# Moving GpSimd's two-operand elementwise work in the second block to VectorE, and the gates' factor on the one-hot rows to ScalarE

## The chip, the cores and the metric

The program runs on one core of one Trainium2 chip. The metric is device time in microseconds (us) for one launch, the median of several runs. The engines are named as in the profile: PE is TensorE (its matmuls; its weight loads are PEld), DVE is VectorE, ACT is ScalarE, POOL is GpSimd, SP is SyncE.

## What is computed

Two transformer blocks in float32 on 256 tokens of width 2048, one after the other. The change touches only the second. It has a mixer (retention and a gated recurrence behind one input product), an attention to 256 memory rows, and a product-key expert layer, cut here to what matters:

```
q  = rmsnorm(h) @ w_q                       # 8 heads x 2 halves of 128
s1 = q1 @ sub_keys1, s2 = q2 @ sub_keys2    # 128 keys each
best 16 of each, best 16 of their sums      # per token and head
gate = softmax over the 16
act  = gelu(rmsnorm(h) @ U)                 # all 16384 experts
h   += (act * gates of all experts) @ V
```

The 128 gates of a token (8 heads x 16) stand in a matrix of 128 x 128 experts: the kernel builds it, token by token, as a product of two one-hot matrices, of which the first is multiplied by the gates.

## The kernel before, in words

Every large product streams its weights. `Stream.run` (L139) goes through all half pieces of weights (128 x 1024 values) in program order. At half piece i, `ahead` (L90) first issues the load of a later piece on SP's queue and the split of half piece i + 4: `split` (L77) has ACT round the raw weights to float32r (`whi`, L84) and another engine take the difference (`wlo`, L87). Then PE gets the matmuls of half piece i (L163 to L165, or L173 and L174 where the weights are stationary), and `steps(2)` (L118) lets the tasks in `side` emit one step each, two steps in all (a step that yields "pause" is not counted). So the order of each engine's queue is fixed when the program is built: split of half i + 4, matmuls of half i, then a little of the other work. Each engine takes its queue in order.

The difference of L87 is VectorE's, except where a product was added with the key `pool`: there every second, third or fourth half piece is GpSimd's. That holds for six of the twelve products behind `w_in_2` (`block2`, 24 half pieces), for the four of `w_q` (`peer`, 16 half pieces), and for the first eight of `peer_u` (17 half pieces), 57 in all.

Three more places use GpSimd for a product or a sum of two tensors in SBUF:

- `normed` (L1461) builds the normalised operand of the experts in eight parts: a sum (L1467) and a product with the row of norms (L1468), 128 x 512 each, then ACT and VectorE split it (L1470, L1471).
- `topk` (L1495), once for each of four pairs of heads, finds the best keys on VectorE (MAX8, FIND_INDEX8, MATCH_REPLACE8) and at its end compares places with 0 to 15 (`eq`, L1552, VectorE) and multiplies by the indices (L1554, GpSimd), 4 x 2 x 4 = 32 times 128 x 256, before a sum (L1558).
- `gates` (L1561) goes through 64 groups of four tokens. `hot(k)` makes the two one-hot matrices `oh` of group k, 128 x 512 each, by two comparisons on VectorE (L1583) and one multiplication of the first by the gates on GpSimd (L1585). In the loop, group k + 2 is made, then PE multiplies group k (L1599, four products of 128 x 128), ACT writes the result to `gst` (L1601), and after every fourth group GpSimd issues two stores to DRAM (L1604). Three groups come in two half pieces. Beside it runs the product `peer_u`, whose end for every four half pieces is `gelu_pair` (L1444): one step on ACT and one on VectorE in each of three half pieces (L1450 and L1451, L1453 and L1454, L1456 and L1457).

Behind the gates, `weigh` (L1610) reads them back from DRAM, multiplies the activations by them (L1626) and splits the product (L1629, L1630), four parts for each sixteenth of the experts.

GpSimd's other work is small: `rsqrt` (L236), one cast in `topk` (L1510), and issuing DMAs.

Of the kernel before, what the change touches and what calls it, by code (L numbers as in the profile page):

```python
# [42 lines left out]
class Stream:  # L43
    """The weight products: pieces of weights are loaded ahead, split ahead into two float32r parts
    whose sum is exact, and multiplied in order, with the steps of other work put in between."""
# [11 lines left out]
    def add(s, **j):  # L57
        """A product: pieces (weights, their blocks of 128 rows, columns, part of the product)."""
        parts = [piece[3] for piece in j["pieces"]]
        for c, piece in enumerate(j["pieces"]):  # L60
            p, u = len(s.pieces), piece[3]
            s.pieces.append(piece[:3])
            nk = len(piece[1])
            cuts = [0, nk] if nk * piece[2] <= 1024 else [0, nk // 2, nk]
            for k0, k1 in zip(cuts, cuts[1:]):
                s.halves.append((j, p, k0, k1, c == 0 and k0 == 0, u, u not in parts[:c] and k0 == 0,
                                 u not in parts[c + 1:] and k1 == nk))
# [9 lines left out]
    def split(s, i):  # L77
# [7 lines left out]
        # where VectorE has much else to do, GpSimd takes a part of the differences  # L85
        e = s.nc.gpsimd if "pool" in j and i % j["pool"] == 0 else s.nc.vector
        e.tensor_tensor(lo[:, :w], raw, hi[:, :w].bitcast(F32), op=ALU.subtract)  # L87
        s.parts[i] = (hi, lo)

    def ahead(s, i):  # L90
        """Loads and splits as far ahead of half piece i as there is room."""
# [8 lines left out]
    def spawn(s, *gens, first=False):  # L100
        """Other work, after the task that is running or before all."""
# [3 lines left out]
    def step(s, g):  # L105
        """One step of a task: whether it did something."""
# [11 lines left out]
    def steps(s, n):  # L118
        """A step each of the first n tasks that have something to do."""
# [61 lines left out]
class Kernel:  # L181
# [16 lines left out]
    def g(self, shape, name, dt=F32):  # L198
        """A tile of the shared store, of at most 4 KB of a partition."""
# [16 lines left out]
    def keep1(self, shape, name):  # L216
        """1 KB of a partition that is kept for long, but not for all of the time."""
# [12 lines left out]
    def rsqrt(self, out, ss, n, eps=EPS):  # L230
        """out = (ss / n + eps) ** -0.5"""
# [6 lines left out]
    def row_bcast(self, out, r, late=1):  # L238
        """A task: out[p, t] = r[t % 128, t // 128] on every partition."""
# [11 lines left out]
    def sumsq(self, out, x, n):  # L251
        """out[p] = the sum of x squared along the free axis."""
# [3 lines left out]
    def turned(self, dst, src, kbs, gain=None):  # L256
        """dst[:, hi/lo, i, tok], the transposed [128 tok, 128] blocks src(m, kb) of two kbs, times
        gain(kb) by row, in two exact parts."""
# [19 lines left out]
    def wparts(self, name, c, late=False):  # L278
        """Of 512 columns, two parts of 256, for a product with the weights stationary; in turns
        where the last rows of the operand come late."""  # L280
# [22 lines left out]
    def attention(self, q, k, bias, v, done, start=None, sums=None, then=None):  # L303
        """q(h, m), k(h, keys), v(h, kt), bias(h, m) give operands; done(m, h0, nh, po, rs) takes the
        products of the unnormalised probabilities and one over their sums, to which sums may add;
        the task then() follows."""
# [50 lines left out]
    def group(self, g, o):  # L357
        """The group norm of o [128, m, 512], into two operand tiles of the next product."""
# [40 lines left out]
    def both(self, o, y, z, scale=1.0):  # L399
        """The two parts of a product with the weights stationary, added."""  # L400
# [3 lines left out]
    def end_w(self, name, scale, R):  # L404
        """The end of a product with the weights stationary: [n, tok] times scale times R by column."""
# [10 lines left out]
    def end_t(self, name, r):  # L416
        """The end of a product with the tokens stationary: [tok, n] times r by row."""
# [8 lines left out]
    def block1(self):  # L426
# [83 lines left out]
        # memory keys and values, kept in DRAM until they are needed  # L510
# [23 lines left out]
    def rel_bias(self):  # L534
        """The relative bias and the masks: bias[h // 4][q, h % 4, j] for the key at distance
        128 + q - j, and the one of the compressed keys."""
# [14 lines left out]
        # the compressed keys lie at distances of which those of the keys are a part, or in the future  # L551
# [23 lines left out]
    def mla_prep(self):  # L575
# [13 lines left out]
        # the rotated shared key  # L589
# [55 lines left out]
    def log1p_exp_neg(self, y, n):  # L645
        """log1p(y) for y in [0, 1], as 2 artanh(y / (2 + y)) by its series, in place."""
# [15 lines left out]
    def log_sigmoid(self, out, z, n):  # L662
        """out = min(z, 0) - log1p(exp(-|z|))"""
# [9 lines left out]
    def fox_gate(self):  # L673
        """The running sums of the gates' logarithms along the tokens, by token and transposed."""
# [77 lines left out]
    def gelu(self, out, x, w, half=True):  # L752
        """out = 2 gelu(x), or gelu(x) with half, for x [128, w] in PSUM or not (tanh form)."""
# [9 lines left out]
    def nsa(self):  # L763
# [8 lines left out]
        for kv in range(2):  # L772
            # the keys (values) of the blocks, flat, and their positions' (in the last column), times
            # the first weights: one product a position, for both groups, one below the other
# [40 lines left out]
        # the gates  # L815
# [5 lines left out]
        # the compressed keys  # L821
# [45 lines left out]
        # the selected blocks (four of four: all of them up to the query), and the window  # L867
# [43 lines left out]
    def residual_end(self, n, src, gain, dst, then=None):  # L911
        """The end of a product whose n-th 512 columns add to h; the new h is squared, and turned
        for the next product with its gain."""
# [98 lines left out]
    def second_norm(self, n, h, hg):  # L1012
        """The first block's last norm and the second's first: hg = h * final_norm is what both
        square, and what the next product takes, with its own gain."""
# [37 lines left out]
    def block2(self):  # L1052
# [48 lines left out]
        for i, (mode, c, end) in enumerate(jobs):  # L1101
            pieces = self.wparts("w_in_2_w", c) if mode == "w" else self.wpieces("w_in_2_t", c)
            more = {"begin": lambda: S.side.extend([self.tables(), self.lru(), self.retention(0), self.retention(1)])}
            S.add(mode=mode, pieces=pieces, x=x, need=need, end=end, **({"pool": 2} if 3 <= i < 9 else {}),
                  **(more if i == 0 else {}))

    def rotate(self, d, name, c, u, y, z):
        """The rotary turn of a product with the weights stationary, and its norm."""
# [16 lines left out]
    def gelu_y(self, c):  # L1125
        """2 gelu of the gate of the recurrence, in place."""
# [78 lines left out]
    def lam(self):  # L1205
        """8 log_sigmoid(lambda), by channel."""
# [180 lines left out]
    LAG = 4  # L1387

    def peer(self):
# [14 lines left out]
        for c in range(4):  # L1404
            S.add(mode="w", pieces=self.wparts("w_q", c, c == 0), x=lambda kb: (self.fT[kb // 2], kb % 2), end=q_end(c),
                  pool=2,
# [27 lines left out]
        for s in range(16 + self.LAG):  # L1434
            if s < 16:
                for u in (2 * s, 2 * s + 1):
                    S.add(mode="w", pieces=self.wparts("peer_u", u), x=lambda kb: (self.fn[kb // 2], kb % 2),
                          end=u_end(u), **({"pool": 3 if u < 2 else 4} if u < 8 else {}),
                          need=lambda kbs: kbs[-1] // 2 in self.fn,
# [4 lines left out]
    def gelu_pair(self, c, u, y, z):  # L1444
        """2 gelu of a part of a product, in turns between the engines."""
# [15 lines left out]
    def normed(self):  # L1461
        """The normalised operand of the experts."""
        nc = self.nc
        yield from self.wait("Rf")
        for e in range(8):
            t, o, x = self.fT[e], self.xe("fn"), self.w([128, 2, 256], "fx")
            nc.gpsimd.tensor_tensor(x, t[:, 0].bitcast(F32), t[:, 1].bitcast(F32), op=ALU.add)  # L1467
            nc.gpsimd.tensor_tensor(x, x, self.Rf[:, None, :].to_broadcast([128, 2, 256]), op=ALU.mult)  # L1468
# [6 lines left out]
    def top16(self, rows):  # L1475
        """For each (v, idx, s): v, idx become the 16 largest of s along the free axis, in order, and
        their places; s is changed. The rows go side by side."""
# [17 lines left out]
    def topk(self, c, q):  # L1495
        """The sixteen best of two heads' product keys, for all tokens."""
# [14 lines left out]
        # the pairs that can be among the best sixteen: with a and b better ones in the two lists,  # L1511
# [171 lines left out]
def _col(v):  # L1683
    """[n * 128] -> [128, n]"""
    return v.reshape(-1, 128).T
# [36 lines left out]
def _rotary():  # L1722
    """cos and sin for the transposed [channel, token] heads of 128, for queries and for keys."""
    half = 64
# [100 lines left out]
```

## Time and profile before

| what | value |
|---|---|
| median of 3 runs | 3584.61 us (3584.1 to 3586.18) |
| profiled execution, its span (first to last instruction) | 3584.7 us |
| PE busy | 3495.4 us (98%) |
| PEld busy | 2965.4 us (83%) |
| DVE busy | 2348.0 us (66%) |
| ACT busy | 1647.2 us (46%) |
| POOL busy | 388.8 us (11%) |
| mean granted TensorE clock | 0.993 |
| HBM traffic | 186 GB/s over the span |

No separate time is given for the profiled execution beside its span, which lies 0.1 us above the median of the runs. A busy share is a mean over stages that differ: POOL is near 0 in most of the span and at 5 to 6 tenths from about 1950 to 2330 us, the same stretch in which DVE is at 9 tenths and PE falls below 9. Busy time of an engine counts an instruction from its start to its end, so it holds what the instruction waited for after its start.

### The profile page before, as it was taken

To read this page: it belongs to the slowest core of one execution; us is meant where nothing else is said; L and a number is where in the kernel's file an instruction comes from. 1 tells how busy PE (TensorE), PEld (TensorE's weight loads), DVE (VectorE), ACT (ScalarE), POOL (GpSimd) and SP (SyncE) were. 2 spreads that over 40 slices of the span, in tenths; PEclk is the share of its full clock that TensorE was granted. 3 is DMA by queue.
4 is the path that set the end of the run, shared out by engine and by line. 5 is a ranking of instruction groups with operands and counts; after the bars stand their busy time and mean duration, and the time that the engine had idled before them with its cause. 6 is when DMAs were issued, how large, how long until landed. Compare 5 with 4: busy or idle time off the path is not lost.

```text
span 3584.7 us, 45859 instructions
## 1 busy us (share of the span) xinstructions
PE 3495.4 (98%) x18204; PEld 2965.4 (83%) x18204; DVE 2348.0 (66%) x3371; ACT 1647.2 (46%) x2298; POOL 388.8 (11%) x319
## 2 busy tenths in 40 slices
PE   9999999999999999999999888899999999999998
PEld 8888888888888888788888677778888888888887
DVE  5565565545555566875556999966666666666765
ACT  5455445444343454445444344444444444444443
POOL 0000000000000002310005556600000000000000
PEclk9999999999999999999999999999999999999999
DMA  6444455555555554455545445655555555555654
GB/s 220 166 143 165 174 189 178 193 188 199 185 197 198 195 197 180 153 176 187 191 153 179 138 157 184 195 205 200 200 200 200 201 201 203 203 202 202 222 210 153
DMA packets 103351, 670.28 MB, mean 187 GB/s; under 512 B 11684, under 2 KB 12469, under 8 KB 30176
## 3 DMA queue, kind: packets, MB, share of 16 engines
q1 hardware_dynamic: 87120, 610.98, 47.8%
q0 software_dynamic: 15728, 56.29, 4.8%
q8 instruction: 143, 2.34, 0.3%
q14 instruction: 72, 0.59, 0.0%
q10 hardware_dynamic: 288, 0.07, 0.0%
HBM read 644.21 MB, written 23.09 MB: 186 GB/s over the span
## 4 chain that ended last, share of the span: by engine, by line
PE 76%; DVE 13%; issue 6%; ACT 2%; POOL 2%; DMA 0%; POOLq 0%; SPq 0%; DVEq 0%; ACTq 0%
PE mm L173 21%; PE mm L163 13%; PE mm L165 13%; PE mm L164 13%; PE mm L174 11%; DVE wlo L87 4%; ACT whi L84 2%; DVE wx L1626 2%; DVE oh L1583 2%; POOL oh L1585 1%; PE ss L315 1%; PE ss L263 1%; PE ss L342 1%; DVE ti L1486 0%; DVE acc L1419 0%
## 5 line engine op out<-in xcount | busy, mean ns | idle before, releaser
L87 DVE TENSOR_TENSOR wlo<-raw,whi 128x1024 fp32r<-128x1024 f32 (+2 forms) x1105 | 1376.4, 1265 | 439.1 <-ACT whi L84 438.0
L84 ACT ACTIVATE whi<-raw 128x1024 fp32r<-128x1024 f32 (+2 forms) x1162 | 1196.6, 1049 | 546.4 <-PE mm L165 473.2
L173 PE MATMUL mm<-xT,whi 128*128 128x512 f32 x2368 | 851.9, 403 | 0.0
L173 PE MATMUL mm<-fn,whi 128*128 128x512 f32 x2048 | 729.0, 399 | 6.1 <-DVE act L1457 4.1
L174 PE MATMUL mm<-xT,wlo 128*128 128x256 f32 x2368 | 668.0, 282 | 9.7 <-DVE wlo L87 9.7
L174 PE MATMUL mm<-fn,wlo 128*128 128x256 f32 x2048 | 578.5, 282 | 17.4 <-DVE wlo L87 13.2
L173 PEld LDWEIGHTS mm<-xT,whi 128*128 128x128 f32 x2368 | 449.0, 190 | 108.0 <-issue 1.4
L173 PEld LDWEIGHTS mm<-fn,whi 128*128 128x128 f32 x2048 | 386.9, 189 | 94.6 <-issue 3.5
L174 PEld LDWEIGHTS mm<-xT,wlo 128*128 128x128 f32 x2368 | 451.2, 191 | 12.4 <-DVE wlo L87 11.5
L174 PEld LDWEIGHTS mm<-fn,wlo 128*128 128x128 f32 x2048 | 389.8, 190 | 24.8 <-DVE wlo L87 19.5
L164 PE MATMUL mm<-wlo,W 128*128 128x512 f32 x1024 | 399.1, 390 | 2.7 <-DVE wlo L87 2.7
L165 PE MATMUL mm<-whi,W 128*128 128x512 f32 x1024 | 398.7, 389 | 0.0
L163 PE MATMUL mm<-whi,W 128*128 128x512 f32 x1024 | 398.5, 389 | 0.0
L164 PEld LDWEIGHTS mm<-wlo,W 128*128 128x128 f32 x1024 | 192.2, 188 | 43.6 <-DVE wlo L87 4.0
L163 PEld LDWEIGHTS mm<-whi,W 128*128 128x128 f32 x1024 | 192.2, 188 | 40.9 <-ACT whi L84 0.6
L165 PEld LDWEIGHTS mm<-whi,W 128*128 128x128 f32 x1024 | 192.2, 188 | 39.8
L163 PE MATMUL mm<-whi,hid 128*128 128x512 f32 x512 | 199.8, 390 | 0.0
L165 PE MATMUL mm<-whi,hid 128*128 128x512 f32 x512 | 199.3, 389 | 0.0
L164 PE MATMUL mm<-wlo,hid 128*128 128x512 f32 x512 | 199.3, 389 | 0.0
L1419 DVE TENSOR_TENSOR acc<-mm,acc 128x512 f32<-128x512 f32 x128 | 82.4, 686 | 175.6 <-PE mm L165 175.6
L87 POOL TENSOR_TENSOR wlo<-raw,whi 128x1024 fp32r<-128x1024 f32 x57 | 144.2, 2530 | 308.3 <-ACT whi L84 307.8
L1629 ACT ACTIVATE W<-wx 128x512 fp32r<-128x512 f32 x64 | 40.5, 632 | 225.0 <-DVE wx L1626 225.0
(505 smaller groups left out, 4196.6 us busy)
## 6 DMA issues: line engine op xcount, KB each, us to landing
raw<-in_peer_u SPq DMA_DIRECT2D x128, 1024.0 KB, 4.9
raw<-in_peer_v SPq DMA_DIRECT2D x128, 1024.0 KB, 4.9
raw<-in_w_up SPq DMA_DIRECT2D x64, 1024.0 KB, 5.0
raw<-in_w_down SPq DMA_DIRECT2D x64, 1024.0 KB, 4.9
raw<-in_w_in_w SPq DMA_DIRECT2D x52, 1024.0 KB, 4.9
raw<-in_w_out SPq DMA_DIRECT2D x32, 1024.0 KB, 4.9
raw<-in_w_in_t SPq DMA_DIRECT2D x22, 1024.0 KB, 4.8
raw<-in_w_xv SPq DMA_DIRECT2D x16, 1024.0 KB, 4.9
```

Of the source, the lines that this page charges most:

```text
L84: s.nc.scalar.activation(hi[:, :w], raw, AF.Copy)
L87: e.tensor_tensor(lo[:, :w], raw, hi[:, :w].bitcast(F32), op=ALU.subtract)
L163: nc.tensor.matmul(o, xh, w, start=st, stop=False, skip_group_check=True)
L164: nc.tensor.matmul(o, xh, v, start=False, stop=False, skip_group_check=True)
L165: nc.tensor.matmul(o, xl, w, start=False, stop=en, skip_group_check=True)
L173: nc.tensor.matmul(o, w[:, c], xt[:, :, kl], start=st, stop=False, skip_group_check=True)
L174: nc.tensor.matmul(o[:, 0], v[:, c], xt[:, 0, kl], start=False, stop=en, skip_group_check=True)
L263: nc.tensor.transpose(p[:, (2 * i + m) * 128:(2 * i + m + 1) * 128], src(m, kb), self.ident)
L1419: nc.vector.tensor_tensor(h[:, m], acc[m], h[:, m], op=ALU.add)
L1583: nc.vector.tensor_tensor(o[i], iota[:, None, :].to_broadcast([128, 4, 128]), tr[i][:, 4 * k:4 * k + 4, None].to_broadcast([128, 4, 128]), ...
L1626: nc.vector.tensor_tensor(x[:, :, 128 * i:128 * i + 128], self.act[2 * s + e // 2][:, 2 * (e % 2):2 * (e % 2) + 2, 128 * i:128 * i + 128], ...
L1629: nc.scalar.activation(t[:, 0], x, AF.Copy)
```

## The change

`split` no longer looks at `pool`: all differences are VectorE's, and the three uses of the key are gone. In `normed`, `topk` and `hot` the GpSimd operations are replaced as shown. Comments and docstrings are removed as well, so a line of the changed kernel has a number lower by 2 to 4 in these places. Cut to its core:

```diff
 def split(s, i):
     s.nc.scalar.activation(hi[:, :w], raw, AF.Copy)
-    e = s.nc.gpsimd if "pool" in j and i % j["pool"] == 0 else s.nc.vector
-    e.tensor_tensor(lo[:, :w], raw, hi[:, :w].bitcast(F32), op=ALU.subtract)
+    s.nc.vector.tensor_tensor(lo[:, :w], raw, hi[:, :w].bitcast(F32), op=ALU.subtract)
...
 # block2
-    S.add(mode=mode, pieces=pieces, x=x, need=need, end=end, **({"pool": 2} if 3 <= i < 9 else {}),
+    S.add(mode=mode, pieces=pieces, x=x, need=need, end=end,
...
 # peer: w_q, then peer_u
-          pool=2,
...
-          end=u_end(u), **({"pool": 3 if u < 2 else 4} if u < 8 else {}),
+          end=u_end(u), need=lambda kbs: kbs[-1] // 2 in self.fn,
...
 # normed
-    nc.gpsimd.tensor_tensor(x, t[:, 0].bitcast(F32), t[:, 1].bitcast(F32), op=ALU.add)
-    nc.gpsimd.tensor_tensor(x, x, self.Rf[:, None, :].to_broadcast([128, 2, 256]), op=ALU.mult)
+    nc.vector.tensor_tensor(x, t[:, 0].bitcast(F32), t[:, 1].bitcast(F32), op=ALU.add)
+    nc.vector.tensor_tensor(x, x, self.Rf[:, None, :].to_broadcast([128, 2, 256]), op=ALU.mult)
...
 # topk
-    nc.gpsimd.tensor_tensor(eq[m][:, h], eq[m][:, h],
+    nc.vector.tensor_tensor(eq[m][:, h], eq[m][:, h],
                             ids[:, m, 2 * h + i, None, :].to_broadcast([128, 16, 16]), op=ALU.mult)
...
 # gates, hot(k)
-    nc.gpsimd.tensor_tensor(o[0], o[0], tr[2][:, 4 * k:4 * k + 4, None].to_broadcast([128, 4, 128]), op=ALU.mult)
+    for j in range(4):
+        nc.scalar.activation(o[0][:, j], o[0][:, j], AF.Copy, scale=tr[2][:, 4 * k + j:4 * k + j + 1])
```

The new factor is one ACTIVATE for each token of the group, 128 x 128, whose scale is a column with one value for each partition; 256 of them for the 64 groups. PE's queue is the same, instruction by instruction. POOL's queue falls from 173 rows to 74, and its last 32 rows are now the stores to `gd`, one behind the other.

How the queues change in the stage of the gates. ACT's queue there, before, over five half pieces (`whi` is the split, `gst` the write of a group's product, `act` a step of `gelu_pair`):

```order
L84 ACTIVATE whi<-raw 128x1024
L1450 ACTIVATE act<-mm 128x512
L1601 ACTIVATE gst<-ss 128x4x8x8 x4
L84 ACTIVATE whi<-raw 128x1024
L1453 ACTIVATE act<-mm 128x512
L1601 ACTIVATE gst<-ss 128x4x8x8 x2
L84 ACTIVATE whi<-raw 128x1024
L1456 ACTIVATE act<-act 128x512
L1601 ACTIVATE gst<-ss 128x4x8x8 x4
L84 ACTIVATE whi<-raw 128x1024
L1601 ACTIVATE gst<-ss 128x4x8x8 x2
L84 ACTIVATE whi<-raw 128x1024
```

and ACT's queue with the change, over two half pieces and the next ones:

```order
L84 ACTIVATE whi<-raw 128x1024
L1446 ACTIVATE act<-mm 128x512
L1582 ACTIVATE oh<-oh,gtr 128x128 x4
L1598 ACTIVATE gst<-ss 128x4x8x8 x2
L1582 ACTIVATE oh<-oh,gtr 128x128 x4
L1598 ACTIVATE gst<-ss 128x4x8x8 x2
L84 ACTIVATE whi<-raw 128x1024
L1449 ACTIVATE act<-mm 128x512
L1582 ACTIVATE oh<-oh,gtr 128x128 x4
L1598 ACTIVATE gst<-ss 128x4x8x8 x2
L84 ACTIVATE whi<-raw 128x1024
L1452 ACTIVATE act<-act 128x512
```

Before each write of `gst` there now stand the four scalings of a group two ahead, and each of them stands in front of the next split `whi`.

VectorE's queue in the same place with the change (before, the same, but without the `wlo` of every fourth half piece):

```order
L1579 TENSOR_TENSOR oh<-cst,gtr 128x512 x4
L85 TENSOR_TENSOR wlo<-raw,whi 128x1024
L1579 TENSOR_TENSOR oh<-cst,gtr 128x512 x2
L85 TENSOR_TENSOR wlo<-raw,whi 128x1024
L1447 TENSOR_TENSOR mm<-mm,act 128x2x256
L1579 TENSOR_TENSOR oh<-cst,gtr 128x512 x4
L85 TENSOR_TENSOR wlo<-raw,whi 128x1024
L1450 SCALAR_TENSOR_TENSOR act<-act,mm 128x512
```

Each comparison that a scaling on ACT needs stands behind the `wlo` of the same half piece, and that behind its `whi`.

## Rows read from the trace of the kernel before

**Rows 1.** Mixer, a gap in it, topk, gates: PE, PEld, DVE, ACT, POOL busy, PEclk, DMA.

```profile
1340.00:1560.00 220.00, 212.75 (x1181) 185.19 (x1180) 171.65 (x238) 103.23 (x136) 67.58 (x29) 0.98 0.47 167
1498.00:1508.00 10.00, 7.97 (x36) 7.06 (x36) 8.15 (x20) 3.74 (x5) 4.26 (x3) 0.66 0.61 211
1930.00:2112.00 182.00, 157.79 (x862) 134.81 (x863) 169.84 (x581) 70.34 (x92) 107.29 (x75) 0.95 0.42 145
2117.00:2326.00 209.00, 185.24 (x1193) 162.13 (x1192) 205.04 (x193) 99.93 (x203) 137.57 (x104) 1.00 0.59 186
```

**Rows 2.** What PE waited for in 2117 to 2326: us, times, longest.

```profile
PE ss L1599 <- POOL oh L1585: 23.8, 32, 1.8
```

**Rows 3.** POOL's groups, whole span: forms, count, busy us, mean ns, idle before.

```profile
L87 POOL TENSOR_TENSOR wlo<-raw,whi 128x1024 fp32r<-128x1024 f32 x57 | 144.2, 2530 | 308.3 <-ACT whi L84 307.8 <-POOL wlo L87 0.4
L1585 POOL TENSOR_TENSOR oh<-oh,gtr 128x512 f32<-128x512 f32 x64 | 87.7, 1370 | 76.1 <-DVE oh L1583 75.9
```

**Rows 4.** DVE's groups in 2117 to 2326, same columns.

```profile
L1583 DVE TENSOR_TENSOR oh<-cst,gtr 128x512 f32<-128x512 f32 x127 | 118.6, 984 | 0.0
L87 DVE TENSOR_TENSOR wlo<-raw,whi 128x1024 fp32r<-128x1024 f32 x33 | 71.8, 2176 | 0.0
```

**Rows 5.** DVE's timeline in the gates: start, us, instruction.

```profile
2224.28 1.28 DVE L1583 TENSOR_TENSOR oh<-cst,gtr 128x512 f32<-128x512 f32 x2
```

**Rows 6.** ACT's timeline: two first steps of `gelu_pair`, ten periods apart.

```profile
2117.94 0.60 ACT L1450 ACTIVATE act<-mm 128x512 f32<-128x512 f32 x1 [3.06 <-PE mm L174]
...
2312.80 0.60 ACT L1450 ACTIVATE act<-mm 128x512 f32<-128x512 f32 x1 [1.17 <-PE mm L174]
```

**Rows 7.** PE's timeline in the gates: a group, a half piece, a group.

```profile
2230.29 1.16 PE L1599 MATMUL ss<-oh 128*128 128x128 f32 x8
2231.21 0.47 PE L173 MATMUL mm<-fn,whi 128*128 128x512 f32 x1
...
2234.07 1.05 PE L1599 MATMUL ss<-oh 128*128 128x128 f32 x8
```

**Rows 8.** DVE's timeline behind the gates, in `weigh`, where POOL is idle.

```profile
2341.48 1.23 DVE L87 TENSOR_TENSOR wlo<-raw,whi 128x1024 fp32r<-128x1024 f32 x1 [0.25 <-ACT whi L84]
2342.62 0.68 DVE L1454 SCALAR_TENSOR_TENSOR act<-act,mm 128x512 f32<-128x512 f32 x1
2343.22 1.17 DVE L1626 TENSOR_TENSOR wx<-act,G 128x256 f32<-128x256 f32 x2
```

**Rows 9.** ACT's timeline, the same stretch.

```profile
2340.41 1.04 ACT L84 ACTIVATE whi<-raw 128x1024 fp32r<-128x1024 f32 x1
...
2344.42 0.63 ACT L1629 ACTIVATE W<-wx 128x512 fp32r<-128x512 f32 x1 [2.49 <-DVE wx L1626]
2344.96 1.04 ACT L84 ACTIVATE whi<-raw 128x1024 fp32r<-128x1024 f32 x1
```

**Rows 10.** ACT's timeline: an exponential with a column operand; two writes of `gst`.

```profile
116.61 0.40 ACT L322 ACTIVATE P<-s,nm 128x128 f32<-128x128 f32 x1 [1.83 <-DVE nm L320]
116.92 0.19 ACT L322 ACTIVATION_READ_ACCUMULATOR P<-s,nm 128x1 f32 x1
...
2236.72 0.66 ACT L1601 ACTIVATE gst<-ss 128x256 f32<-128x256 f32 x2 [0.90 <-PE ss L1599]
2237.26 1.06 ACT L84 ACTIVATE whi<-raw 128x1024 fp32r<-128x1024 f32 x1
```

**Rows 11.** DVE's groups in 1930 to 2112, columns as in rows 3.

```profile
L87 DVE TENSOR_TENSOR wlo<-raw,whi 128x1024 fp32r<-128x1024 f32 x30 | 49.1, 1635 | 1.8 <-ACT whi L84 1.7
L1552 DVE TENSOR_TENSOR eq<-qs,cst 128x256 f32<-128x256 f32 x32 | 22.1, 750 | 0.0
```

**Rows 12.** DVE's groups in 1340 to 1560, and POOL's in 1930 to 2112.

```profile
L87 DVE TENSOR_TENSOR wlo<-raw,whi 128x1024 fp32r<-128x1024 f32 x45 | 64.2, 1441 | 5.2 <-ACT whi L84 5.1
...
L1244 DVE TENSOR_TENSOR xc<-xc,ig 128x256 f32<-128x256 f32 x8 | 3.4, 420 | 9.8 <-ACT ig L1243 9.8
...
L87 POOL TENSOR_TENSOR wlo<-raw,whi 128x1024 fp32r<-128x1024 f32 x19 | 49.1, 2584 | 28.0 <-ACT whi L84 28.0
```

More of the change, by code (lines that the diff above doesn't have):

```diff
@@ L1437, in peer @@
                     S.add(mode="w", pieces=self.wparts("peer_u", u), x=lambda kb: (self.fn[kb // 2], kb % 2),
-                          end=u_end(u), **({"pool": 3 if u < 2 else 4} if u < 8 else {}),
-                          need=lambda kbs: kbs[-1] // 2 in self.fn,
+                          end=u_end(u), need=lambda kbs: kbs[-1] // 2 in self.fn,
                           **({"begin": lambda: S.side.append(self.gates())} if u == 0 else {}))
```

## The prediction

> **What bounds the kernel now.** Read first the busy shares and their slices: PE is at 98%, so outside a few stretches nothing but PE's own work counts. Then busy time by stretch finds the stretches [rows 1]. In the mixer PE is idle for 220 - 212.75 = 7.3 us, in topk for 182 - 157.8 = 24.2 us, in the gates for 209 - 185.2 = 23.8 us. The change can give back no more than these, about 55 us, and a little for clock: the granted clock is 0.95 in topk and 1.00 in the gates.
>
> Next, who is late. In the gates all of PE's wait is for GpSimd's factor on the one-hot rows [rows 2]. But VectorE is busy for 205 of 209 us there, and the reader should see that much of this is no work: a comparison of 128x512 has a mean of 984 ns and a split difference 2176 ns [rows 4], where two comparisons in a row with GpSimd idle take 1.28 us, one of them 0.68 with a step of 0.60 [rows 5], and a difference behind the gates, GpSimd idle, takes 1.23 us [rows 8]. So VectorE stands still while GpSimd multiplies two tensors: (984 - 680) ns x 127 + (2176 - 1230) ns x 33 = 39 + 31 = 70 us of its 205.
>
> The pace before: `gelu_pair` begins every four half pieces, and ten of these periods, 60 groups, go from 2117.94 to 2312.80 [rows 6], 19.49 us a period. PE's own need is less: a half piece from 2231.21 to 2234.07 is 2.86 us, a group from 2230.29 to 2231.21 is 0.92 us [rows 7]. Four half pieces and six groups make 11.44 + 5.52 = 16.96 us.
>
> **The gates.** Removed from GpSimd are 64 factors of 1.37 us and the differences of 2.53 us [rows 3]; VectorE loses the 70 us of standing still and gains 10 differences at 1.23 = 12 us. Its own need falls to 205 - 70 + 12 = 147 us, well below PE's. That is the gain, and it is a large one on paper.
>
> What is added is 256 ACTIVATEs on ACT, and what matters is where they stand. In ACT's queue a half piece is now: `whi`, a step of `gelu_pair`, four scalings, two writes of `gst`, in every second half piece four more scalings and two more writes, then the next `whi`. In VectorE's: `wlo`, a step of `gelu_pair`, the comparisons. The scalings wait for the comparison, the comparison stands behind `wlo`, `wlo` waits for `whi`, and the next `whi` stands behind the scalings. This is a closed loop through two in-order queues, from one `whi` to the next, that no other buffer loosens. Before, the factor lay on GpSimd, and ACT's queue held nothing that waited for a comparison of the same half piece.
>
> Such a loop exists already behind the gates. From `whi` to `whi` it is 2340.41 to 2344.96 = 4.55 us [rows 9], and its pieces add up to that: `whi` to `wlo` 1.07, `wlo` 1.14 by its step to the next, the step of `gelu_pair` 0.60 [rows 8], two products 1.17 and 0.03 to ACT, ACT's step 0.54 [rows 9]. ACT stood idle 2.49 us of it, VectorE also waited, and a half piece of PE's would have taken 2.86.
>
> The new loop by the same pieces. The first comparison: 0.68 + 0.03. A scaling of 128x128 with a column operand: the nearest row is an exponential of the same shape with a column as bias, 0.40 us with 0.31 us to the start of the next instruction [rows 10]; I take 0.31, so 1.24 for four. The two writes take 2237.26 - 2236.72 = 0.54 [rows 10]. A half piece with one group and no gelu step: 1.07 + 1.14 + 0.71 + 1.24 + 0.54 = 4.70. A gelu step adds 0.60; a second group adds 1.24 + 0.54 = 1.78, its comparisons being done meanwhile. The period has half pieces of 7.08 (two groups, gelu), 5.30 (one, gelu), 7.08 and 4.70: 24.16 us against 19.49. PE, with 16.96, waits. 64 groups are 10.67 periods: 10.67 x 4.67 = **+50 us**.
>
> Ends for the scaling: a write of `gst` of 256 columns has a step of 0.27 [rows 10], so half the columns are at least 0.14; without any overlap it is 0.40. The period is then 20.1 or 26.3 us, the term +6 or +73. I stay with 0.31, since shape, type and number of operands are those of the row.
>
> Stores: with GpSimd free they are issued when `gst` is written; GpSimd had time for them before, so nothing.
>
> **Topk.** VectorE is busy 169.8 of 182 us [rows 1]. Gone is standing still of at least (1635 - 1230) x 30 = 12.2 us in the differences and (750 - 420) x 32 = 10.6 us in the comparisons [rows 11], with 420 ns for 128x256 [rows 12]. Added are 19 differences [rows 12] at a step of 1.14 = 21.7, 32 products of 128x256 at 0.42 = 13.4, and 16 operations of 128x512 from `normed` at 0.68 = 10.9, together 46.0 us. The sum, 169.8 - 22.8 + 46.0 = 193, is 11 us over the stretch. VectorE is still the bound here and PE, with 24 us idle, does not cover it. Groups whose stalls I have not counted lower this, products that depend on the comparison just before them do not. Ends 0 and +11; I take **+8 us**, nearer the upper end because a full queue has nothing to give back.
>
> **Mixer.** 24 differences are moved, 24 x 1.23 = 29.5 us, of which VectorE's shorter differences alone give (1441 - 1230) x 45 = 9.5 back [rows 12]. At most 171.7 + 20 = 192 of 220 us: cover remains, and `wlo` is made four half pieces ahead. Nothing, with ends of -7 (PE's idle time there gone) and +7 (as much again).
>
> **Sum.** 3584.7 (span of the profiled execution, 0.1 above the median of the runs) + 50 + 8 + 0 = 3642.7, on the runs' scale 3642.6 us.
>
> **Rivals.** *Faster, PE sets the pace.* VectorE no longer stands still, and PE goes through the gates at its own 16.96 us a period: 10.67 x (16.96 - 19.49) = -27 us; if topk also gains from the freed engine, say nothing lost there, 3558 us. For it: the 70 us are real, and ACT has the room by its sum (99.9 of 209 us busy [rows 1], 64 x 1.24 = 79 more). Against it: the order of the queues; without the scalings the loop is 24.16 - 24 x 0.31 = 16.7, so the change is a gain only if a scaling costs less than (19.49 - 16.72) / 24 = 0.115 us, below the lower end. Chance 0.08. The Trainium skill, page SBUF — State Buffer, section "SBUF: two separate sides", has a rule that speaks for this rival: VectorE operations with two SBUF inputs and GpSimd operations that read SBUF take one shared port pair as an exclusive lock, while ACT's ports wait for no one. By that rule alone the sum would end near 3558. The trace agrees with the lock (680 ns against 984).
>
> *No change.* Loop and gain cancel: the scaling near 0.12 us and topk at 0. Chance 0.04.
>
> *Worse, TensorE's clock.* The scalings that release PE follow each other by up to 7.1 us, and PE's work in between is 2 x 0.92 + 2.86 = 4.7, so single waits reach 2.4 us. In ten microseconds of the mixer where PE was busy for 7.97, the granted clock is 0.66 [rows 1], where 1.00 is 2.4 GHz and 0.5 is 1.2 GHz. PE has room down to 16.96 / 24.16 = 0.70; at 0.66 the period is 25.7 us (3659 us in all), at 0.5 throughout 33.9 us (3746 us). Against it: a PE that slows is idle less. Chance 0.04.
>
> **How the numbers follow.** The loop has 0.84: 3643 us, with 3584 to 3676 if all ends of the terms fall together; 3605 to 3672 leaves out only the far ends and half of the clock's case. Faster 0.08 (the first rival), same 0.04, slower 0.88 (loop and clock); 0.2%, some 7 us, is about what a measurement of this kernel can tell from no change.
>
> **What would show it.** After the change, in the gates: a period of about 24 us between the first steps of `gelu_pair`; ACT idle before the first scaling of a half piece, released by the comparison; VectorE idle before `wlo`, released by `whi`; comparisons near 0.68 and differences near 1.23 us; PE's wait for the scaled rows near 10.67 x (24.16 - 16.96) = 77 us instead of 23.8. In topk VectorE nearly without gaps, and PE's waits for `wlo` a little longer. Wrong if ACT has no idle time there, if the period is under 19.5, or if the mixer moves by more than 7 us.

## The result and the profile after

| what | value |
|---|---|
| after, median of 4 runs | 3631.12 us (3629.76 to 3632.53) |
| before, median of 4 runs beside it | 3584.97 us (3584.1 to 3586.18) |
| ratio | 1.0125, 95% interval 1.0113 to 1.0138 |
| span of the profiled execution | 3628.1 us, mean granted TensorE clock 0.995 |

The kernel is slower by 46.2 us; 3642.6 with a range of 3605 to 3672 was predicted. (The ratio is the estimate on record; the two medians alone give 1.0129.) The page of after, its first and second parts (the two rows of slices that matter here):

```profile
PE 3491.0 (96%) x18204; PEld 2961.4 (82%) x18204; DVE 2304.1 (64%) x3476; ACT 1716.1 (47%) x2554; POOL 105.3 (3%) x150
...
PE   9999999999999999999999777789999999999998
POOL 0001000000000000000000001000000000000000
```

GpSimd is almost empty and VectorE has less busy time than before, yet PE has four slices at 7 tenths: slices 23 to 26, of 90.7 us each, so from about 2000 to 2360 us.

PE's instructions are the same in the same order, so the two traces can be laid beside each other at the same matmul. Spans differ by 3628.1 - 3584.7 = 43.4 us, and they come about here (start of a matmul after, less its start before):

| stretch of before | difference at its end | gained or lost |
|---|---|---|
| start to 200 us | -1.5 | -1.5 |
| 200 to 1340 | -1.45 | 0 |
| 1340 to 1930 (mixer and behind it) | -7.5 | -6.1, of it -3.8 between 1470 and 1480 |
| 1930 to 2117 (topk) | -0.7 | +6.8 |
| 2117 to 2326 (gates) | +41.6 | +42.4 |
| 2326 to 2345 | +43.5 | +1.9 |
| 2345 to the end | +43.4 | 0 |

The first two rows lie ahead of everything that the change touches; the other kernels below stand at -1.8 to +2.8 us at 1340, so the -1.5 is not put down to the change.

Busy time by stretch after, in the order PE, PEld, DVE, ACT, POOL, PEclk, DMA share, GB/s: the mixer as in [rows 1], then topk and the gates each between the same two matmuls as 1930.49 to 2117.03 and 2117.03 to 2326.04 before:

```profile
1340.00:1560.00 220.00, 215.86 (x1203) 188.01 (x1202) 175.12 (x267) 107.16 (x142) 5.47 (x3) 0.98 0.47 166
...
1922.96:2116.30 193.34, 161.88 (x887) 137.38 (x886) 185.99 (x658) 72.07 (x96) 5.33 (x7) 0.96 0.42 144
2116.30:2367.66 251.36, 186.10 (x1193) 162.52 (x1192) 146.62 (x201) 168.44 (x455) 26.49 (x30) 1.00 0.47 153
```

In the gates VectorE's busy time fell from 205 us to 146.6 as the argument had it (147), PE's own stayed at 186, and the stretch grew from 209 to 251 us. No engine is full: the time is in waits. What PE waited for in the gates of after (total us, times, longest), where [rows 2] had GpSimd:

```profile
PE ss L1596 <- ACT oh L1582: 63.7, 41, 2.2
PE ss L1596 <- DVE oh L1579: 1.5, 1, 1.5
```

ACT's and VectorE's groups in 2117 to 2370 of after, which answer to [rows 4] (count, busy us, mean ns, idle before and what ended it):

```profile
L1582 ACT ACTIVATE oh<-oh,gtr 128x128 f32<-128x128 f32 x253 | 80.7, 391 | 82.9 <-DVE oh L1579 82.9
```

```profile
L1579 DVE TENSOR_TENSOR oh<-cst,gtr 128x512 f32<-128x512 f32 x126 | 79.3, 685 | 0.0
L85 DVE TENSOR_TENSOR wlo<-raw,whi 128x1024 fp32r<-128x1024 f32 x43 | 52.7, 1226 | 105.3 <-ACT whi L84 105.3
```

ACT stands idle for 82.9 us for VectorE's comparisons, VectorE for 105.3 us for ACT's `whi`, and PE for what both make. One period of ACT's queue shows why (ACT's timeline of after: start, us, instruction, idle before it):

```profile
2235.77 1.05 ACT L84 ACTIVATE whi<-raw 128x1024 fp32r<-128x1024 f32 x1
2236.72 0.58 ACT L1446 ACTIVATE act<-mm 128x512 f32<-128x512 f32 x1
2239.31 1.28 ACT L1582 ACTIVATE oh<-oh,gtr 128x128 f32<-128x128 f32 x4 [2.01 <-DVE oh L1579]
2240.49 0.63 ACT L1598 ACTIVATE gst<-ss 128x256 f32<-128x256 f32 x2
2241.02 1.27 ACT L1582 ACTIVATE oh<-oh,gtr 128x128 f32<-128x128 f32 x4
2242.19 0.64 ACT L1598 ACTIVATE gst<-ss 128x256 f32<-128x256 f32 x2
2242.72 1.06 ACT L84 ACTIVATE whi<-raw 128x1024 fp32r<-128x1024 f32 x1
...
2247.98 1.05 ACT L84 ACTIVATE whi<-raw 128x1024 fp32r<-128x1024 f32 x1
...
2254.94 1.05 ACT L84 ACTIVATE whi<-raw 128x1024 fp32r<-128x1024 f32 x1
...
2259.60 1.05 ACT L84 ACTIVATE whi<-raw 128x1024 fp32r<-128x1024 f32 x1
2260.55 0.59 ACT L1446 ACTIVATE act<-mm 128x512 f32<-128x512 f32 x1
```

and VectorE's in the same half piece:

```profile
2236.85 1.23 DVE L85 TENSOR_TENSOR wlo<-raw,whi 128x1024 fp32r<-128x1024 f32 x1 [2.23 <-ACT whi L84]
2237.99 0.69 DVE L1447 TENSOR_TENSOR mm<-mm,act 128x512 f32<-128x512 f32 x1
2238.59 2.49 DVE L1579 TENSOR_TENSOR oh<-cst,gtr 128x512 f32<-128x512 f32 x4
2243.81 1.23 DVE L85 TENSOR_TENSOR wlo<-raw,whi 128x1024 fp32r<-128x1024 f32 x1 [2.73 <-ACT whi L84]
```

Follow the hand-over: `whi` at 2235.77 releases `wlo` at 2236.85, behind it the step of `gelu_pair` and then the first of four comparisons at 2238.59, whose end releases the scalings at 2239.31, and behind the scalings and the writes of `gst` stands the next `whi` at 2242.72. From one `whi` to the next these are 6.95, 5.26, 6.96 and 4.66 us, where the prediction had 7.08, 5.30, 7.08 and 4.70. The period, from L1446 to L1446, is 23.83 us here and (2355.84 - 2141.42) / 9 = 23.82 over nine of them; 24.16 was predicted and 19.49 is before's.

### The profile page after: what moved, and what is told of

Same layout as the page of the kernel before. It is cut to its first block, busy times and chain, and to the rows that moved or that the text cites. A ratio compares the mean times of both kernels' runs of the same rounds, so it can differ in the third digit from the quotient of the medians.

```text
span 3628.1 us, 45998 instructions
## 1 busy us (share of the span) xinstructions
PE 3491.0 (96%) x18204; PEld 2961.4 (82%) x18204; DVE 2304.1 (64%) x3476; ACT 1716.1 (47%) x2554; POOL 105.3 (3%) x150
## 4 chain that ended last, share of the span: by engine, by line
PE 76%; DVE 11%; issue 6%; ACT 6%; DMA 0%; POOL 0%; DVEq 0%; SPq 0%; POOLq 0%; ACTq 0%
PE mm L171 21%; PE mm L161 13%; PE mm L162 13%; PE mm L163 13%; PE mm L172 11%; DVE wlo L85 4%; ACT whi L84 3%; ACT oh L1582 2%; DVE wx L1623 2%; PE ss L313 1%; ACT gst L1598 1%; DVE oh L1579 1%; PE ss L261 1%; PE ss L340 1%; DVE acc L1416 0%
## 5 line engine op out<-in xcount | busy, mean ns | idle before, releaser
L85 DVE TENSOR_TENSOR wlo<-raw,whi 128x1024 fp32r<-128x1024 f32 (+2 forms) x1162 | 1391.2, 1217 | 551.7 <-ACT whi L84 550.6
L1596 PE MATMUL ss<-oh 128*128 128x128 f32 x512 | 70.7, 281 | 65.3 <-ACT oh L1582 63.7
```

The costliest lines, as they stand in the source:

```text
L85: s.nc.vector.tensor_tensor(lo[:, :w], raw, hi[:, :w].bitcast(F32), op=ALU.subtract)
L1596: nc.tensor.matmul(p[:, j * 128:(j + 1) * 128], o[0][:, j], o[1][:, j], start=True, stop=True)
```

## The experiments

The theory: the closed loop through two in-order queues makes the gates slow (the loop theory). Its rivals: ACT simply has too much to do with 256 more instructions (the load theory), or VectorE is too slow with GpSimd's work (the VectorE theory). Every ratio below is to the kernel before, run on the same chip beside it; before took 3586.39 us beside the first four experiments, 3590.64 beside the next four and 3584.79 beside the last two, so times of different series are compared by their distance from before. The expectation of each run stands as it was written before the run.

### The factor back on GpSimd, the rest of the change kept

```diff
 # after, gates, hot(k)
-    for j in range(4):
-        nc.scalar.activation(o[0][:, j], o[0][:, j], AF.Copy, scale=tr[2][:, 4 * k + j:4 * k + j + 1])
+    nc.gpsimd.tensor_tensor(o[0], o[0], tr[2][:, 4 * k:4 * k + 4, None].to_broadcast([128, 4, 128]), op=ALU.mult)
```

> The changed kernel with the factor on the one-hot rows back on GpSimd, all else as changed. Loop theory (a scaling on ACT that waits for VectorE's comparison closes a loop from whi to whi): the loop is gone, the period of the gates falls from 23.8 us to 17 to 19.5, most likely 18.8, since VectorE needs 13.8 and still stands still beside 6 factors a period; about 3578 us in all, 3562 to 3590. Load theory (ACT has too much work with 256 more ACTIVATEs): the same. VectorE theory (the work moved to VectorE is what costs): the period stays above 22 us, over 3610 us in all.

Measured: 3581.82 us, ratio 0.9984 (0.9974 to 0.9994), 4.6 us less than before. The period is (2309.17 - 2121.09) / 10 = 18.81 us. VectorE's groups in 2125 to 2290 of this kernel:

```profile
L1579 DVE TENSOR_TENSOR oh<-cst,gtr 128x512 f32<-128x512 f32 x105 | 81.2, 823 | 0.0
L85 DVE TENSOR_TENSOR wlo<-raw,whi 128x1024 fp32r<-128x1024 f32 x35 | 75.1, 2144 | 0.0
```

All of VectorE's new work is still there, and the whole loss is gone. The VectorE theory falls: the loss hangs on the factor's place. Loop and load theory expected the same here, so this run does not part them. The differences again take 2144 ns in place of 1226, now with GpSimd multiplying only the one-hot rows.

### The factor on VectorE

```diff
 # after, gates, hot(k)
-    for j in range(4):
-        nc.scalar.activation(o[0][:, j], o[0][:, j], AF.Copy, scale=tr[2][:, 4 * k + j:4 * k + j + 1])
+    nc.vector.tensor_tensor(o[0], o[0], tr[2][:, 4 * k:4 * k + 4, None].to_broadcast([128, 4, 128]), op=ALU.mult)
```

> The changed kernel with the factor as one product of 128x512 on VectorE. Loop theory: VectorE's own work sets the pace, a period of 12 x 0.60 + 6 x 0.68 + 4 x 1.14 + 3 x 0.60 = 17.6 us against PE's 16.96; 3631 - 10.67 x 6.2 = 3565 us. Load theory for ACT: the same. VectorE theory: slower than the factor on GpSimd, over 3610 us.

Measured: 3561.84 us, ratio 0.9933 (0.9916 to 0.9949), period 17.15 us. Busy time in 2125 to 2290 of this kernel, columns as above:

```profile
2125.00:2290.00 165.00, 161.16 (x1078) 146.14 (x1077) 165.00 (x240) 90.59 (x183) 25.26 (x29) 1.00 0.64 214
```

VectorE, with more work than in the change, has no gap at all, and PE is nearly full. So the engine on which the change put the factor is what made it slower, but this run alone leaves open whether ACT was overloaded or only badly ordered.

### The same instructions on ACT, one group later

The comparisons of group k + 3 are now issued where those of k + 2 were, and the scalings stay with group k + 2, so that each scaling finds its comparison done in an earlier turn. ACT has the same 256 scalings.

```diff
 # after, gates
+        def scale(k):
+            o = oh[k]
             for j in range(4):
                 nc.scalar.activation(o[0][:, j], o[0][:, j], AF.Copy, scale=tr[2][:, 4 * k + j:4 * k + j + 1])
...
         hot(1)
+        scale(0)
+        hot(2)
+        scale(1)
         for k in range(64):
...
+            if k < 61:
+                hot(k + 3)
             if k < 62:
-                hot(k + 2)
+                scale(k + 2)
```

> The changed kernel, the same 256 ACTIVATEs on ACT, but each group's scalings are issued one group after its comparisons, so that they wait only for comparisons that are long done. Loop theory: the order was the cost, not the work; the period falls to 17 to 18 us, PE's or ACT's own need (16.96 and about 15.6), so 3631 - 10.67 x 6.3 = 3563 us, 3556 to 3572. Load theory: ACT has the same work, the period stays at 23 to 24 us and the time at 3625 to 3635 us.

Measured: 3556.21 us, ratio 0.9913 (0.9897 to 0.993), period 16.58 us. Busy time in 2125 to 2290 of this kernel, columns as above:

```profile
2125.00:2290.00 165.00, 165.00 (x1121) 151.03 (x1120) 139.28 (x191) 157.70 (x432) 26.55 (x30) 1.00 0.66 220
```

ACT's group of scalings in the same stretch, before which ACT stood idle for 82.9 us in the gates of the change:

```profile
L1585 ACT ACTIVATE oh<-oh,gtr 128x128 f32<-128x128 f32 x240 | 76.8, 400 | 2.8 <-DVE oh L1579 2.7
```

and a piece of its ACT timeline:

```profile
2210.79 1.29 ACT L1585 ACTIVATE oh<-oh,gtr 128x128 f32<-128x128 f32 x4
2211.96 0.67 ACT L1606 ACTIVATE gst<-ss 128x256 f32<-128x256 f32 x2
2212.90 1.29 ACT L1585 ACTIVATE oh<-oh,gtr 128x128 f32<-128x128 f32 x4 [0.27 <-DVE oh L1579]
2214.09 0.63 ACT L1606 ACTIVATE gst<-ss 128x256 f32<-128x256 f32 x2
2214.62 1.05 ACT L84 ACTIVATE whi<-raw 128x1024 fp32r<-128x1024 f32 x1
```

The longest wait for a comparison in this piece is 0.27 us where it was 2.01, all such waits in the 165 us come to 2.7, ACT gets 432 instructions into 165 us, and PE has no gap in the stretch. Of the change itself the row of busy times is

```profile
2125.00:2290.00 165.00, 121.33 (x778) 105.86 (x777) 97.06 (x133) 109.76 (x299) 17.67 (x20) 1.00 0.47 153
```

with 299 instructions on ACT and PE idle for 44 us. The load theory falls: the same work in another order is some 75 us faster than the change. This is the run that shows the loop as the cause. The period of 16.58 us lies below the 17 to 18 that were expected, and below the 16.96 that the prediction had for PE alone from one half piece and one group: with PE busy without a gap, 16.58 is PE's own need, and 16.96 was 0.38 us too much.

### Only the factor on ACT

```diff
 # before, gates, hot(k)
-    nc.gpsimd.tensor_tensor(o[0], o[0], tr[2][:, 4 * k:4 * k + 4, None].to_broadcast([128, 4, 128]), op=ALU.mult)
+    for j in range(4):
+        nc.scalar.activation(o[0][:, j], o[0][:, j], AF.Copy, scale=tr[2][:, 4 * k + j:4 * k + j + 1])
```

> The kernel before with the factor alone moved to ACT; the differences of one half piece in four, normed and topk stay on GpSimd. Loop theory: where GpSimd takes the difference, VectorE's comparison waits for no whi and the loop is cut in that half piece, some 2.2 us less a period, while VectorE stands still a little beside GpSimd: a period of 21.5 to 23 us, 3606 to 3622 us. Load theory: the whole cost of the gates is there, 3625 to 3632 us.

Measured: 3637.98 us, ratio 1.0144 (1.0127 to 1.0161), period 24.37 us. A miss. The expectation held that the loop is cut in the half piece whose difference GpSimd takes, because VectorE's comparisons then stand behind no `wlo`. VectorE's timeline there, in this kernel:

```profile
2212.47 1.29 DVE L1583 TENSOR_TENSOR oh<-cst,gtr 128x512 f32<-128x512 f32 x2
2216.47 0.70 DVE L1451 TENSOR_TENSOR mm<-mm,act 128x512 f32<-128x512 f32 x1 [2.71 <-ACT act L1450]
2217.08 3.75 DVE L1583 TENSOR_TENSOR oh<-cst,gtr 128x512 f32<-128x512 f32 x4
2223.55 1.23 DVE L87 TENSOR_TENSOR wlo<-raw,whi 128x1024 fp32r<-128x1024 f32 x1 [2.72 <-ACT whi L84]
```

and ACT's:

```profile
2214.90 1.05 ACT L84 ACTIVATE whi<-raw 128x1024 fp32r<-128x1024 f32 x1
2215.85 0.58 ACT L1450 ACTIVATE act<-mm 128x512 f32<-128x512 f32 x1
2219.06 1.28 ACT L1586 ACTIVATE oh<-oh,gtr 128x128 f32<-128x128 f32 x4 [2.62 <-DVE oh L1583]
```

There is no `wlo` on VectorE here, but the half piece has a step of `gelu_pair`: L1451 waits for L1450, and L1450 stands behind `whi` on ACT. The loop closes through that step in place of `wlo`. And GpSimd's difference makes four comparisons take 3.75 us where they take 2.49 otherwise, so this half piece takes 2222.46 - 2214.90 = 7.56 us, against 6.95 in the change (the next `whi` is at 2222.46). The way by the step is shorter: the comparisons begin 2.18 us behind `whi`, against 2.82. But the first scaling follows them by 1.98 us where it was 0.72, and GpSimd's difference runs from 2216.09 to 2218.47 us, into them. The next three half pieces take 5.26, 6.96 and 4.66 us, as in the change, so the longer period lies in this half piece. That GpSimd's difference is what slows these comparisons was read from the trace; no run took it or the step away. The granted clock is below 1.00 in this stage:

```profile
2125.00:2290.00 165.00, 125.16 (x765) 109.28 (x764) 94.06 (x122) 108.02 (x289) 32.72 (x27) 0.96 0.46 149
```

But the half piece from 2214.90 to 2222.46 ran at 0.82 and the same one a period later, 2239.34 to 2246.89, at 1.00, and that takes 7.55 us: the clock does not set the period here.

### Only the mixer's differences on VectorE

```diff
 # before, block2
-    S.add(mode=mode, pieces=pieces, x=x, need=need, end=end, **({"pool": 2} if 3 <= i < 9 else {}),
+    S.add(mode=mode, pieces=pieces, x=x, need=need, end=end,
```

> The kernel before with only the 24 differences of the mixer moved to VectorE. My first theory gave this 0 us. The traces of before and change, laid side by side at the same matmul of PE, show the change 5.6 us ahead after the mixer: if that is the moved differences' doing (VectorE's stalls beside GpSimd delayed what PE waited for), 3586 - 5.5 = 3581 us, and PE's two waits near 1473 and 1499 us shrink; if it is chance, 3586 us.

Measured: 3585.83 us, ratio 0.9987 (0.9977 to 0.9996), 4.8 us less than before beside it. At the same matmuls it gains 3.84 us between 1470 and 1480 and 5.6 from 1440 to 1560. The two kernels that leave the mixer as before (the experiments before and behind this one) differ from before by no more than 0.2 us there. Behind the mixer this trace gives back more than 5 us, 4.2 of them from 2326 us to the end, where it has the same instructions as before; the trace of before is from another series, and the 4.8 us of the runs are the measure. What PE waited for in 1340 to 1560 of before, of which the second row has no counterpart in this kernel:

```profile
PE ss L1175 <- DVE st L1166: 4.7, 2, 2.8
PE mm L174 <- DVE wlo L87: 2.6, 2, 2.1
```

Before, VectorE and GpSimd take a difference at nearly the same moment there. VectorE's timeline of before, and GpSimd's:

```profile
1471.46 3.41 DVE L87 TENSOR_TENSOR wlo<-raw,whi 128x1024 fp32r<-128x1024 f32 x1
```

```profile
1471.18 2.61 POOL L87 TENSOR_TENSOR wlo<-raw,whi 128x1024 fp32r<-128x1024 f32 x1 [3.36 <-ACT whi L84]
```

and PE's, of before:

```profile
1474.93 0.38 PE L174 MATMUL mm<-xT,wlo 128*128 128x256 f32 x1 [2.05 <-DVE wlo L87]
```

VectorE's difference begins 0.28 us after GpSimd's and takes 3.41 us where it takes 1.23 with GpSimd idle: GpSimd's ends 2.33 us after VectorE's began, and the rest is about one difference alone. PE waits for it. Behind this wait the granted clock falls, and from 1476.26 to 1479.47 us PE's pairs of matmuls follow each other by 0.64 us in place of 0.35. Of the 3.84 us, 2.3 are gained up to 1475.15, by the wait, and 1.5 behind it, by the clock. The window 1472 to 1482, of before and then of this kernel:

```profile
1472.00:1482.00 10.00, 7.95 (x37) 6.64 (x36) 9.90 (x9) 5.03 (x6) 4.66 (x3) 0.83 0.30 107
```

```profile
1472.00:1482.00 10.00, 10.00 (x58) 8.68 (x57) 9.80 (x15) 5.15 (x6) 0.00 (x0) 1.00 0.51 191
```

Without GpSimd's differences both this wait and the fall in the clock behind it are gone.

### Only topk's work on VectorE

The differences of `w_q` and of the first two parts of `peer_u`, the two operations of `normed` and the product of `topk`, as in the change; the mixer and the gates as before.

```diff
 # before, peer
-    pool=2,
...
-    end=u_end(u), **({"pool": 3 if u < 2 else 4} if u < 8 else {}),
+    end=u_end(u), **({"pool": 4} if 2 <= u < 8 else {}),
...
 # normed (both operations) and topk
-    nc.gpsimd.tensor_tensor(
+    nc.vector.tensor_tensor(
```

The port theory of the expectation says that GpSimd's operations hold VectorE up for about as long as they take on VectorE itself.

> The kernel before with only the operations of normed, topk, the differences of w_q and of the first two products of peer_u moved to VectorE. Own-work theory: VectorE is the bound there and gets more work than its stalls give back, + 7 us as the traces show it, 3593 us. Port theory: what GpSimd did cost VectorE as much, within 2 us of before.

Measured: 3596.04 us, ratio 1.0015 (1.0006 to 1.0024), 5.4 us more than before, by the interval 2.2 to 8.6, which just leaves out the port theory's 2 us. Its trace loses 4.8 us between 1930 and 2117, so the loss is topk's own and needs nothing from the gates.

### Versions that put the parts together

The mixer's and the gates' differences on VectorE, topk's work left on GpSimd; the factor on VectorE in the first, on ACT one group later in the second.

```diff
 # before, block2 and peer_u, both versions
-    S.add(mode=mode, pieces=pieces, x=x, need=need, end=end, **({"pool": 2} if 3 <= i < 9 else {}),
+    S.add(mode=mode, pieces=pieces, x=x, need=need, end=end,
...
-    end=u_end(u), **({"pool": 3 if u < 2 else 4} if u < 8 else {}),
+    end=u_end(u), **({"pool": 3} if u < 2 else {}),
```

> A combination: the mixer's differences on VectorE, topk and normed on GpSimd as before, in the gates the factor and all differences on VectorE. Terms: mixer -5.5, gates 10.67 x (17.15 - 19.49) = -25, topk 0: 3586 - 30.5 = 3555 us. If topk costs nothing by the move (port theory), the same as with topk moved, 3562 us.

Measured: 3562.68 us, ratio 0.992 (0.9907 to 0.9934), 28.0 us less than before. The terms had 30.5 and the port theory 24, both within the interval, so this run does not decide on topk.

> The same, but the factor on ACT with the scalings one group later. Terms: mixer -5.5, gates 10.67 x (16.58 - 19.49) = -31, topk 0: 3586 - 36.5 = 3549.5 us. Under the port theory for topk the same as with topk moved, 3556 us.

Measured: 3556.06 us, ratio 0.9902 (0.9887 to 0.9917), 34.6 us less than before; the terms had 36.5, the port theory 30, and again both lie within the interval. This and the third experiment differ only in topk, but were measured in different series, and their intervals overlap, so both were run again side by side. First the one with topk moved, then the one with topk kept:

> The whole change with the scalings of a group issued one group after its comparisons, as in the third experiment, now beside the version that keeps topk on GpSimd. If the separate measurements add up, this one is slower by what topk's move costs, 5 to 7 us: ratio to before near 0.991 to 0.992. If topk's cost disappears once the gates follow at PE's pace (the gates' own wait then taking up topk's delay), the two are equal within 2 us.

> The mixer's differences on VectorE, topk left on GpSimd, the gates' work as in the change but with the scalings one group later. If the separate measurements add up: ratio to before 0.990, 5 to 7 us below its companion with topk moved. If topk's cost disappears in the gates, equal to it within 2 us.

Measured: 3558.25 us (3553.76 to 3560.18), ratio 0.9923 (0.9909 to 0.9936), with topk moved, and 3550.28 us (3548.97 to 3550.64), ratio 0.9903 (0.9888 to 0.9919), with topk kept. The two ranges of times do not meet, though the intervals of the ratios still overlap. At the same matmuls, from 1930 to 2117 of before, the first loses 6.7 us against before and the second 1.5, and in the gates both gain 31.9. So topk's move costs 5.2 us of the 8.6 between the two spans and is not hidden by what follows; 2.8 of the rest lie in the first 500 us, where the kernels are the same and which no change explains. Topk on GpSimd and the scalings one group later is the best version found: faster than before by 34.5 us and than the change by about 81.

## Why the prediction was right

**The gates: right, in mechanism and size.** +50 was predicted, and +42.4 measured, with 1.9 more behind the last group. Of the loop's pieces only the scaling was a little smaller than taken. Four scalings and the step to the next instruction are 2240.49 - 2239.31 = 1.18 us, 0.295 each, against 0.31; that is 24 x 0.015 = 0.36 us of a period, and 24.16 - 23.82 is 0.34. At 10.67 periods the pace alone would make 10.67 x (23.82 - 19.49) = 46 us; the 4 us less lie at the two ends of the stage and were not followed up. Of the signs: comparisons 685 ns (0.68), differences 1226 ns (1.23), ACT idle before the first scaling for the comparison, VectorE idle before `wlo` for `whi`. All came. PE's wait was 63.7 + 1.5 = 65.2 us, where 77 was predicted; the shorter period is 10.67 x 0.34 = 3.6 us of this. Of the other 8, about 5 are PE's busy time, 186.1 us in the stretch where 10.67 x 16.96 makes 181.0, and about 3 the ends, as the stretch is 251.4 us long and 10.67 x 23.82 makes 254.2. In topk PE's waits for `wlo` went from 18.3 to 21.9 us, a little longer as forecast.

**The break-even of a scaling, 0.115 us,** was the argument against the faster rival. It was right for the order of this change. It is no property of ACT: with the scalings one group later the same 0.295 us cost PE no wait in 165 us.

**Rival, PE sets the pace.** False of the change, and true of the mended order: 3558 was its time, and the third experiment is at 3556.21. That the two are so near is in part luck: in that trace the gates gain 31.9 us where the rival had 27, the mixer gains 6.1, and topk costs 6.6 where the rival had nothing for both. The Trainium skill, page SBUF — State Buffer, section "SBUF: two separate sides", where the rule stands that speaks for it (an exclusive lock between GpSimd operations that read SBUF and VectorE operations with two SBUF inputs), agrees with these traces: VectorE stands still no longer, a comparison takes 685 ns where it took 984, and 205 us became 146.6. What the freed engine is worth was decided by the queues.

**Rival, no change.** False: it needed a scaling near 0.12 us.

**Rival, TensorE's clock.** Its waits came (41 of up to 2.2 us, 2.4 predicted), but the granted clock is 1.00 throughout the gates. PE worked 186 of 251 us there at the full 2.4 GHz level. In the fourth experiment, with nearly the same waits (41 of up to 2.2 us), the clock was 0.96, and the period shows no cost of it.

**Topk: right, a little large.** +8 was taken, +6.8 came, and 5.4 with topk alone. Of before, the stretch between the same two matmuls is

```profile
1930.49:2117.03 186.54, 162.82 (x884) 139.11 (x885) 174.38 (x591) 72.87 (x95) 107.03 (x74) 0.95 0.43 147
```

VectorE's busy time rose by 185.99 - 174.38 = 11.6 us and its idle time fell from 12.2 to 7.4. The prediction's sum had a rise of 193 - 169.8 = 23 us: half of this was paid back by groups whose stalls had not been counted, as it said they might be; the eight differences of `normed` alone went from 10.9 to 5.5 us. The end of +11 came from a full queue, and 7 us of gaps remained.

**Mixer: the size was off.** The step "cover remains, and `wlo` is made four half pieces ahead", worth nothing, failed; the change gains 5.5 us in the stretch of 1340 to 1560 and 0.6 up to topk, near the end of -7 that was kept for the range. The sum of busy time over 220 us was right (VectorE 175.1, under the bound of 192), and the cover did hold in most places: four of VectorE's differences take 3.4 us there, each beside one of GpSimd's (at 1409, 1433, 1444 and 1471 us). But at the fourth of them it did not hold: PE waits 2.05 us for it, and the clock falls behind the wait. A mean over 220 us does not show a wait of 2 us; the list of PE's waits of that stretch does, as shown with the fifth experiment.

**The sum.** +58 predicted on the span, 43.4 measured: 42.4 + 1.9 (gates) + 6.8 (topk) - 6.1 (mixer) - 1.5 (the first block) = 43.5. Of the 14.6 us between them the gates' 50 against 44.3 are 5.7, the mixer 6.1, topk 1.2 and the start 1.5.

## What to carry to other kernels

Before moving an operation to another engine, write out what stands before and behind it in that engine's queue, and follow each wait back: if the operation waits for another engine, and that engine's next input stands behind the operation in the same queue, the two queues close a loop, and the loop's length can set the pace, however idle the engines are. Add up the pieces of such a loop from the trace, since their sum gave the period here to 0.34 us of 24. Then look for an order in which the operation's input is a turn older: this stage lost 44 us in one order and gained 32 in the other, with the same work on ACT.

## What the runs showed of the hardware that was not expected

- The one-hot factor alone is enough for GpSimd to slow VectorE's differences: with it there and nothing else to multiply or subtract on GpSimd they had a mean of 2144 ns, and 1226 without. In the mixer a single overlap made a difference of 1.23 us into one of 3.41.
- That stall is shown as VectorE's busy time, not as a wait: VectorE seemed full in the gates of before (205 of 209 us) with some 135 us of work (205 less the prediction's 70 us of standing still; the 147 us after hold ten differences more).
- PE idle for a quarter of 251 us, in 42 waits of up to 2.2 us, kept the granted clock at 1.00, while a wait of 2.05 us in the mixer was followed by a clock of 0.83 in the ten microseconds around it, and 41 waits of up to 2.2 us in the gates of the fourth experiment went with 0.96. Why the one and not the other was not tried.
